# Values phase of a dilated-attention kernel: four token tiles renewed and one key rotation issued later, and the last pair's probabilities read back on SyncE's queue

## The chip, the cores and the metric

The kernel runs on one core of one Trainium2 chip (trn2). The metric is the device time of one execution in microseconds (us); a kernel is timed in several runs and the median counts. A profiled execution is taken beside the timed ones, and all rows of the profile below come from that single execution. Engines are named as the profile names them: PE (TensorE matrix products), PEld (its weight loads), DVE (VectorE), ACT (ScalarE), POOL (GpSimd) and SP (SyncE, which here only issues DMA transfers). Each engine works through its own instructions in the order in which they were placed; they meet through semaphores.

## What is computed

The reference is a two-layer network on 512 tokens of width 1024: dilated attention and a SwiGLU feed-forward layer, then an mLSTM mixer and a second feed-forward layer, with RMS norms. The change touches the attention alone:

```python
proj = (xn @ w_in).reshape(B, S, N_GROUPS, 3, ATTN_HEADS, ATTN_HEAD_DIM)   # 3 groups; q, k, v; 8 heads of 128
for g, (window, dilation) in enumerate(DIL_CONFIGS):                        # (128,1), (512,4), (2048,16)
    q = apply_partial_rope(proj[:, :, g, 0], positions) * scale             # the first 32 of 128 rows are rotated
    k = apply_partial_rope(proj[:, :, g, 1], positions)
    v = proj[:, :, g, 2]
    o, lse = dilated_window_attention(q, k, v, window, dilation)
...
wts = jax.nn.softmax(jnp.stack(lses), axis=0)                               # the three groups share one softmax
o = jnp.einsum('gbsh,gbshd->bshd', wts, jnp.stack(outs))
return o.reshape(B, S, ATTN_WIDTH) @ w_out
```

Here xn is the normalized input; the three groups' results are weighted together, multiplied by w_out and added to the residual h.

## The kernel before

**Products in three parts.** All large products are made with operands split into a high part (fp32r) and a remainder: for a weight tile ACT copies the high part (line 210, tiles ending in _h) and DVE subtracts it from the raw tile (line 211, _l); for activations lines 225/226 and 228/229 do the same. Each product is then three matmuls (`SPLITS`): high times high, low times high, high times low. Every weight goes DMA on SP's queue, then ACT, then DVE, then PE, three buffers deep (`W_BUFS`); `Feed` (line 263) prepares two weight tiles ahead of the one in use.

**Order of the work.** The program is written down in one order, and a scheduler then places each instruction on its engine's list. `behind(fn, engine=...)` and `run(fn)` tie a step's instructions to the last one on an engine; `defer(n, fn)` postpones a step by n ticks, where each chunk of a projection (`project`, line 246) is one tick. So the position of a step in the text moves it on its engine's list, and other instructions may be placed before it.

**First pair's projections.** The eight heads go in four pairs. `project_pair` (line 773) makes q and k of a pair for the three groups. For each, `evac` (line 786) multiplies the accumulator by the cosines (line 790) and shuffles the rows to be rotated out of it (line 574); `rotate` (line 576) multiplies them by the sines (line 577) and adds them (line 582). In pair 0 the tokens are used unnormalized (tiles xa_h, xa_l of x times the gain), and the normalization is applied at each evacuation. While pair 0 is projected, `normalize` writes the normalized tokens to tiles xn, `sum_of` makes the sums S1 to S4 of token blocks, and `renew` (line 828) overwrites the eight operand tiles xa_h (ACT, line 831) and xa_l (DVE, line 832) from xn. `renew(range(4))` is deferred into the last key projection (a0g2k, group 2, part 1); `renew(range(4, 8))` is written right behind that projection, after `rotate` of those keys.

**Values phase.** `values_phase` (line 931) then computes the values of the remaining heads in two units (v0..., v1...). Each unit multiplies tokens by weights through seven block products, in the order P1, P5, P2, P6, P7, P3, P4, each in two halves of 12 matmuls (`multiply_values`, line 974, matmuls on line 982). P1 uses token tiles 0 to 3, P2 tiles 4 to 7, P5 the sum S1. The right-hand sides are made by `prepare_values` (line 903): P5's is W12 - W11, a DVE subtraction on line 907 that must precede ACT's copy (line 210) and DVE's remainder (line 211). `finish` copies accumulators out on ACT (line 939). In the profile v0c is the accumulator of P1 and P2, v0p that of P5, v0u that of P6; the program's weight tiles are v0P_0_h, v0P_1_h and so on (0 and 1 are the halves), their raw tiles v0W. W12 is loaded on SP's queue (line 900) into the place of xn tiles 0 and 1, so its first half waits until tokens 0 and 1 are renewed, its second half for tokens 2 and 3.

**Last pair's attention.** `attention_pair` (line 591) makes the scores, the softmax and the weighting by `joint` and `weigh`. `transposes(i)` (line 730) turns head i's probabilities in blocks on DVE (line 734, tile a3pB for the last pair) and writes them to DRAM (a3pD) in four transfers of 240 KB on POOL's queue (line 737). `bring(i)` (line 740) reads them back as one tile a3pT of 960 KB, also on POOL's queue (line 742). `values(i)` multiplies them (lines 752 and 757, accumulator a3o). In the last pair the steps are, on one tick: `joint` and `weigh(0)`, `transposes(0)`, `bring(0)` and `weigh(1)`, `transposes(1)`, `bring(1)`. A `bring` waits for its head's four writes, and POOL's queue is served in order, so what stands behind it on that queue waits too. Meanwhile PE works on the output product: `out_part` (line 1053) multiplies heads 0 to 5 by w_out (accumulators awo, weights awo_k), then `values(0)`, one more part, `values(1)`, and the rest.

Of the kernel before, what the change touches and what calls it, by code (L numbers as in the profile page):

```python
# [23 lines left out]
HEADS = 8  # L24
# [48 lines left out]
def tile_hybrid_dilated_attn_mlstm(  # L73
# [4 lines left out]
    nc = tc.nc  # L78
    x = x[0]
# [304 lines left out]
    with ExitStack() as actx:  # L384
# [206 lines left out]
        def attention_pair(pr, qks):  # L591
# [6 lines left out]
            p, p0, p12 = [], [], []  # L598
            pts, vt, weight = {}, [], []

            def places():
                p.extend(ap2.tile([P, 15, P], F32, tag="p", name="%sp%d" % (nm, i), bufs=3) for i in range(2))
                p0.extend(t[:, :7] for t in p)
                p12.extend(t[:, 7:] for t in p)
# [45 lines left out]
            def scores12(qk1, qk2):  # L650

                for i in range(2):
                    for g, (q, k) in ((1, qk1), (2, qk2)):
                        sp = score_bank(i, "%ss%d" % (nm, g))
                        for c in range(4):
                            sl = slice(c * P, (c + 1) * P)
                            nc.tensor.matmul(sp[:, sl], q[:, i, sl], k[:, i, sl], start=True, stop=True)
                        for c in range(4):
                            sl = slice(c * P, (c + 1) * P)
                            nc.vector.tensor_tensor_reduce(  # L660
                                p12[i][:, 4 * (g - 1) + c, :], sp[:, sl], mask_causal if g == 1 else mask_dil,
                                1.0, -3e38, op0=ALU.add, op1=ALU.max, accum_out=mx[:, g - 1, i, c:c + 1])
                    exponentials(1, i)
# [73 lines left out]
                    nc.gpsimd.dma_start(d.rearrange("b j a x -> a j b x")[a],  # L737
                                        t[R * a:R * (a + 1)].rearrange("p b n i -> p b (n i)"))

            def bring(i):  # L740
                pt = ap2.tile([P, 4, 15, R], F32, tag="pt", name=nm + "pT", bufs=2)
                nc.gpsimd.dma_start(pt.rearrange("p a n i -> p (a n i)"), pts[i].rearrange("b j a x -> (b j) (a x)"))
                pts[i] = pt

            def values(i, out=None):
# [19 lines left out]
            def first_rest():  # L765
                joint()
                weigh(0)
            rest = (first_rest, lambda: transposes(0), lambda: (bring(0), weigh(1)), lambda: transposes(1),
                    lambda: bring(1))
            return (lambda: (places(), scores0(*qks[0])), lambda: scores12(*qks[1:]), rest, values, load_values,  # L770
                    value_tiles)

        def project_pair(pr, qks, then=None):
            nm = "a%d" % pr
            ct, sines = (ropc, ropes) if pr == 0 else (cosn, sinn)
            late = []
            for g in range(3):
                base = g * 3 * D + pr * 256
                qk = []
                qks.append(qk)  # L780
                for part in range(2):
                    t = tok_tile("%sg%d_%s" % (nm, g, "qk"[part]))

                    sh = ap.tile([R, 2, SEQ], F32, tag="rt", name="rot", bufs=2)

                    def evac(m, acc, t=t, sh=sh, g=g):
                        if g == 0:
                            nc.vector.tensor_tensor(in_order(t[:, m]), by_block(acc), by_block(ct), op=ALU.mult)
                        else:
                            nc.vector.tensor_tensor(t[:, m], acc, ct, op=ALU.mult)  # L790
                        rope_part(sh, m, acc)
                    first = pr == 0 and g == 0 and part == 0
                    if first:
                        def first_evac(evac=evac):
                            bc_hook()
                            for m in range(2):
                                evac(m, facc[m])
                        defer(1, first_evac)
                        late.append((t, sh))
                    else:  # L800
                        if pr == 0 and g == 2 and part == 1:
                            defer(1, lambda: renew(range(4)))
                        project(pair, w_in, base + part * D, KC, evac, "%sg%d%s" % (nm, g, "qk"[part]), ready=feed)
                        while late:
                            rotate(*late.pop(), True, sines)
                        rotate(t, sh, g == 0, sines)
                    qk.append(t)
                    if pr == 0 and 1 <= g:
                        step = 2 * (g - 1) + part
                        (lambda: sum_of("S3"), lambda: sum_of("S4"), lambda: None, lambda: renew(range(4, 8)))[step]()  # L810
                        for key in ((), ("W12", "W22"), (), ())[step]:
                            for hf in range(2):
                                behind(load_block, 0, key, hf, engine=mybir.EngineType.SP)
                if g == 0 and then is not None:
                    then()
                if g == 0 and pr == 0:
                    first_values()
# [113 lines left out]
        def values_phase():  # L931
            bank = lambda tag, name: [ps.tile([P, 512], F32, tag=tag, name=name, bufs=3 if tag == "acc" else 2)
                                      for _ in range(2)]
            target = {"P1": "c11", "P2": "c11", "P5": "p5", "P3": "p5", "P6": "u", "P7": "u", "P4": "u"}
            acc, out = {}, {}

            def copy(to, src):
                for m in range(2):
                    nc.scalar.activation(to[m] if isinstance(to, list) else to[:, m], src[m], AF.Copy)

            def add(to, src):
                for m in range(2):
                    nc.vector.tensor_tensor(to[:, m], src[m], to[:, m], op=ALU.add)

            def stored(u, tile_, half, n):
                nc.gpsimd.dma_start(vD[UNITS[u][n]][half * HALF:(half + 1) * HALF].rearrange("(m p) f -> p m f", p=P), tile_)

            def finish(u, name):
                nm = "v%d" % u
                if name == "P1":  # L950
                    acc["u"] = bank("acc", nm + "u")
                    copy(acc["u"], acc["c11"])
                elif name == "P5":
                    out["v5"] = ap.tile([P, 2, SEQ], F32, tag="rt", name=nm + "v5", bufs=2)
                    copy(out["v5"], acc["p5"])
                elif name == "P6":
                    out["u2"] = ap.tile([P, 2, SEQ], F32, tag="rt", name=nm + "u2", bufs=2)
                    copy(out["u2"], acc["u"])
                elif name == "P2":
                    t = place("st0", nm + "c11")  # L960
                    copy(t, acc["c11"])
                    stored(u, t, 0, 0)
                elif name == "P7":
                    add(out["v5"], acc["u"])
                    stored(u, out["v5"], 1, 1)
                elif name == "P3":
                    add(out["u2"], acc["p5"])
                    stored(u, out["u2"], 0, 1)
                else:
                    t = place("st1", nm + "c21")  # L970
                    copy(t, acc["u"])
                    stored(u, t, 1, 0)

            def multiply_values(u, name, hf):
                nm = target[name]
                if name in ("P1", "P5") and hf == 0:
                    acc[nm] = bank({"c11": "s", "p5": "o"}[nm], "v%d%s" % (u, nm))
                whl = feed.pop()
                for m in range(2):
                    for k in range(2):  # L980
                        for a, b in SPLITS:
                            nc.tensor.matmul(acc[nm][m], left(name, a, 2 * hf + k, m), whl[b][:, k, :],
                                             start=(name in ("P1", "P5") and hf == 0 and k == 0 and (a, b) == SPLITS[0]),
                                             stop=(hf == 1 and k == 1 and (a, b) == SPLITS[-1]), skip_group_check=True)
            for item in items:
                multiply_values(*item)
                if item[2] == 1:
                    finish(*item[:2])

        items = [(u, name, hf) for u in range(len(UNITS)) for name in ORDER for hf in range(2)]  # L990
        plan = [lambda ch=ch: wide_chunk(v12_parts(0), ch, "a0g12v") for ch in range(1, 4)]
# [28 lines left out]
        for pr in range(1, HEADS // 2):  # L1020
# [2 lines left out]
            follow(todo, RUN_AT)  # L1023
            project_pair(pr, qks, lambda fn=following[0]: defer(SCORES0_AT, lambda: run(fn)))
            todo = following
        last_values = todo[3]
        follow(todo, LAST_AT)
        v12 = todo[5]()

# [29 lines left out]

        head_split = lambda k, op: split_act(pair[0][k], pair[1][k], op, None)  # L1060
        for c in range(3):
            out_part(c, feed.pop(), 0)
        whl = [feed.pop() for _ in range(3)]
        for i in range(2):
            out_part(i, whl[i], 1, (0, 1))
# [1061 lines left out]
```

## Time and profile before

| What | Value |
|---|---|
| timed runs | 1399.1, 1401.89, 1403.12 us; median 1401.89 us |
| the profiled execution's own time | 1402.21 us |
| its span, first to last instruction | 1400.3 us |
| mean granted TensorE clock | 0.998 |
| DVE busy | 1120.6 us (80%) |
| ACT busy | 703.1 us (50%) |
| POOL busy | 153.7 us (11%) |
| HBM traffic | 163.63 MB read, 18.87 MB written |

The profile gives busy time by engine, groups of instructions by line, the waits by who ended them, and a timeline in us from the span's start. In a timeline row stand the start, the length, the engine, the line, the operation, output<-inputs, the shapes and a count; in brackets the engine's idle time before it and what ended that. The time of a row xN spans N instructions. DVE and ACT instructions overlap slightly, so the step from one start to the next is shorter than one instruction's length. Buffer numbers are left out of names.

### The profile page before, as it was taken

To read this page: it belongs to the slowest core of one execution; us is meant where nothing else is said; L and a number is where in the kernel's file an instruction comes from. 1 tells how busy PE (TensorE), PEld (TensorE's weight loads), DVE (VectorE), ACT (ScalarE), POOL (GpSimd) and SP (SyncE) were. 2 spreads that over 40 slices of the span, in tenths; PEclk is the share of its full clock that TensorE was granted. 3 is DMA by queue.
4 is the path that set the end of the run, shared out by engine and by line. 5 is a ranking of instruction groups with operands and counts; after the bars stand their busy time and mean duration, and the time that the engine had idled before them with its cause. 6 is when DMAs were issued, how large, how long until landed. Compare 5 with 4: busy or idle time off the path is not lost. (4 is left out here: it accounts for less than half of the span.)

```text
span 1400.3 us, 21529 instructions
## 1 busy us (share of the span) xinstructions
PE 1381.8 (99%) x8308; PEld 1232.1 (88%) x8308; DVE 1120.6 (80%) x1904; ACT 703.1 (50%) x1153; POOL 153.7 (11%) x225
## 2 busy tenths in 40 slices
PE   9999999999999999999999999999999999999997
PEld 7887888888888888999999998898888899999886
DVE  7977769596867299877877898898858987888887
ACT  5325552132325155445566464786534544458854
POOL 1000011111010000000000100113101230001212
PEclk9999999999999999999999999999999999999999
DMA  7533255537262547333253643324334563335963
GB/s 226 165 120 106 99 157 174 150 111 213 88 193 80 181 137 164 121 121 109 92 166 87 156 131 91 92 77 106 97 116 117 136 190 121 121 108 134 196 164 100
DMA packets 136830, 186.00 MB, mean 133 GB/s; under 512 B 8532, under 2 KB 104340, under 8 KB 136728
## 3 DMA queue, kind: packets, MB, share of 16 engines
q1 hardware_dynamic: 117312, 134.17, 30.9%
q0 software_dynamic: 17760, 49.34, 15.3%
q8 instruction: 65, 1.06, 0.3%
q10 hardware_dynamic: 1656, 1.12, 0.2%
q14 instruction: 37, 0.30, 0.1%
HBM read 163.63 MB, written 18.87 MB: 130 GB/s over the span
## 5 line engine op out<-in xcount | busy, mean ns | idle before, releaser
L1430 POOL DMA_DIRECT2D f1T<-in_ffn_w_out_dram x15 | 17.8, 1185 | 209.3 <-DMA f1P_2w_w<-in_ffn_w_out_dram 136.6
L1405 POOL DMA_DIRECT2D f0S<-in_ffn_w_out_dram x10 | 8.7, 891 | 244.8 <-DMA f0S<-in_ffn_w_out_dram 190.9
L1962 POOL DMA_DIRECT2D hD<-hB x32 | 21.7, 697 | 68.4 <-DVE hB L1959 68.4
L241 PE MATMUL mo<-n_h,mo_k_l 128*128 128x512 f32 x64 | 25.3, 396 | 0.0
L241 PE MATMUL mo<-n_h,mo_k_h 128*128 128x512 f32 x64 | 25.2, 394 | 0.0
L241 PE MATMUL mo<-n_l,mo_k_h 128*128 128x512 f32 x64 | 25.2, 394 | 0.0
L241 PE MATMUL mqk<-n_h,mqk_k_h 128*128 128x512 f32 x64 | 25.1, 393 | 0.0
L241 PE MATMUL mwo<-yo_l,mwo_k_h 128*128 128x512 f32 x64 | 25.1, 392 | 0.0
L241 PE MATMUL awo<-ao_h,awo_k_h 128*128 128x512 f32 x64 | 25.1, 392 | 0.0
L241 PE MATMUL mqk<-n_l,mqk_k_h 128*128 128x512 f32 x64 | 25.1, 392 | 0.0
L241 PE MATMUL f1j<-n_h,f1j_h 128*128 128x512 f32 x64 | 25.0, 391 | 0.0
L241 PE MATMUL f0j<-n_h,f0j_h 128*128 128x512 f32 x64 | 25.0, 391 | 0.0
L241 PE MATMUL mwo<-yo_h,mwo_k_l 128*128 128x512 f32 x64 | 25.0, 391 | 0.0
L241 PE MATMUL mqk<-n_h,mqk_k_l 128*128 128x512 f32 x64 | 25.0, 390 | 0.0
L241 PE MATMUL f0j<-n_h,f0j_l 128*128 128x512 f32 x64 | 24.9, 390 | 0.0
L241 PE MATMUL f1j<-n_h,f1j_l 128*128 128x512 f32 x64 | 24.9, 390 | 0.0
L241 PE MATMUL awo<-ao_h,awo_k_l 128*128 128x512 f32 x64 | 24.9, 389 | 0.0
L241 PE MATMUL f0j<-n_l,f0j_h 128*128 128x512 f32 x64 | 24.9, 389 | 0.0
L241 PE MATMUL f1j<-n_l,f1j_h 128*128 128x512 f32 x64 | 24.9, 389 | 0.0
L241 PE MATMUL awo<-ao_l,awo_k_h 128*128 128x512 f32 x64 | 24.9, 389 | 0.0
L241 PE MATMUL mwo<-yo_h,mwo_k_h 128*128 128x512 f32 x64 | 24.8, 391 | 0.0
L211 DVE TENSOR_TENSOR v1P_l<-v1W,v1P_h 128x1024 fp32r<-128x1024 f32 x14 | 17.1, 1224 | 9.6 <-ACT v1P_h L210 9.6
(2492 smaller groups left out, 5670.5 us busy)
## 6 DMA issues: line engine op xcount, KB each, us to landing
f0j_w<-in_ffn_w_in_dram SPq DMA_DIRECT2D x17, 512.0 KB, 5.5
f1j_w<-in_ffn_w_in_dram SPq DMA_DIRECT2D x17, 512.0 KB, 6.1
f1T<-in_ffn_w_out_dram POOLq DMA_DIRECT2D x15, 512.0 KB, 7.6
f0hid<-in_ffn_w_in_dram SPq DMA_DIRECT2D x9, 512.0 KB, 5.7
f1hid<-in_ffn_w_in_dram SPq DMA_DIRECT2D x9, 512.0 KB, 5.2
v0W<-in_attn_w_in_dram SPq DMA_DIRECT2D x8, 512.0 KB, 5.3
v1W<-in_attn_w_in_dram SPq DMA_DIRECT2D x8, 512.0 KB, 4.0
awo_k_w<-in_attn_w_out_dram SPq DMA_DIRECT2D x8, 512.0 KB, 5.0
```

Of the source, the lines that this page charges most:

```text
L211: nc.vector.tensor_tensor(lo[:, :n], raw[:, :n], hi[:, :n].bitcast(F32), op=ALU.subtract)
L241: nc.tensor.matmul(acc, whl[a][:, k, m * P:(m + 1) * P], pairs[b][kk], start=(kk == 0 and (a, b) == SPLITS[0]), stop=(kk == nk - 1 and (a, ...
L1405: nc.gpsimd.dma_start(t, src[1][:, ks], accum_op=ALU.add)
L1430: nc.gpsimd.dma_start(view(to), weight_rows(hk * UNITS + u, n), accum_op=ALU.add)
L1962: nc.gpsimd.dma_start(hD[k // 4].rearrange("(b i) x -> i b x", i=R)[:, :, c0:c0 + R], t[R * a_:R * (a_ + 1)])
```

## The change

The change has three parts. The renewal of token tiles 4 to 7 moves from behind the last key projection to behind the first item of the values phase (P1's first half). The rotation of the last keys (group 2 of pair 0) moves behind the fourth item (P5's second half). In the last pair the five steps become one that leaves out both `bring`; these are called while the output product's first halves are started, `bring(0)` ahead of the second and `bring(1)` ahead of the third, and go on SP's queue.

```diff
--- before.py
+++ after.py
@@ -737,9 +737,9 @@
                     nc.gpsimd.dma_start(d.rearrange("b j a x -> a j b x")[a],
                                         t[R * a:R * (a + 1)].rearrange("p b n i -> p b (n i)"))
 
-            def bring(i):
+            def bring(i, queue=nc.gpsimd):
                 pt = ap2.tile([P, 4, 15, R], F32, tag="pt", name=nm + "pT", bufs=2)
-                nc.gpsimd.dma_start(pt.rearrange("p a n i -> p (a n i)"), pts[i].rearrange("b j a x -> (b j) (a x)"))
+                queue.dma_start(pt.rearrange("p a n i -> p (a n i)"), pts[i].rearrange("b j a x -> (b j) (a x)"))
                 pts[i] = pt
 
             def values(i, out=None):
@@ -767,8 +767,12 @@
                 weigh(0)
             rest = (first_rest, lambda: transposes(0), lambda: (bring(0), weigh(1)), lambda: transposes(1),
                     lambda: bring(1))
+            if pr == HEADS // 2 - 1:
+                rest = (lambda: (first_rest(), transposes(0), weigh(1), transposes(1)),)
             return (lambda: (places(), scores0(*qks[0])), lambda: scores12(*qks[1:]), rest, values, load_values,
-                    value_tiles)
+                    value_tiles, bring)
+
+        postponed = []
 
         def project_pair(pr, qks, then=None):
             nm = "a%d" % pr
@@ -803,11 +807,14 @@
                         project(pair, w_in, base + part * D, KC, evac, "%sg%d%s" % (nm, g, "qk"[part]), ready=feed)
                         while late:
                             rotate(*late.pop(), True, sines)
-                        rotate(t, sh, g == 0, sines)
+                        if pr == 0 and g == 2 and part == 1:
+                            postponed.append(lambda: rotate(t, sh, False, sines))
+                        else:
+                            rotate(t, sh, g == 0, sines)
                     qk.append(t)
                     if pr == 0 and 1 <= g:
                         step = 2 * (g - 1) + part
-                        (lambda: sum_of("S3"), lambda: sum_of("S4"), lambda: None, lambda: renew(range(4, 8)))[step]()
+                        (lambda: sum_of("S3"), lambda: sum_of("S4"), lambda: None, lambda: None)[step]()
                         for key in ((), ("W12", "W22"), (), ())[step]:
                             for hf in range(2):
                                 behind(load_block, 0, key, hf, engine=mybir.EngineType.SP)
@@ -982,10 +989,14 @@
                             nc.tensor.matmul(acc[nm][m], left(name, a, 2 * hf + k, m), whl[b][:, k, :],
                                              start=(name in ("P1", "P5") and hf == 0 and k == 0 and (a, b) == SPLITS[0]),
                                              stop=(hf == 1 and k == 1 and (a, b) == SPLITS[-1]), skip_group_check=True)
-            for item in items:
+            for i, item in enumerate(items):
                 multiply_values(*item)
                 if item[2] == 1:
                     finish(*item[:2])
+                if i == 0:
+                    renew(range(4, 8))
+                if i == 3:
+                    postponed.pop()()
 
         items = [(u, name, hf) for u in range(len(UNITS)) for name in ORDER for hf in range(2)]
         plan = [lambda ch=ch: wide_chunk(v12_parts(0), ch, "a0g12v") for ch in range(1, 4)]
@@ -1023,7 +1034,7 @@
             follow(todo, RUN_AT)
             project_pair(pr, qks, lambda fn=following[0]: defer(SCORES0_AT, lambda: run(fn)))
             todo = following
-        last_values = todo[3]
+        last_values, last_bring = todo[3], todo[6]
         follow(todo, LAST_AT)
         v12 = todo[5]()
 
@@ -1059,7 +1070,10 @@
 
         head_split = lambda k, op: split_act(pair[0][k], pair[1][k], op, None)
         for c in range(3):
-            out_part(c, feed.pop(), 0)
+            whl = feed.pop()
+            if c:
+                last_bring(c - 1, nc.sync)
+            out_part(c, whl, 0)
         whl = [feed.pop() for _ in range(3)]
         for i in range(2):
             out_part(i, whl[i], 1, (0, 1))
```

## Prediction

> **What bounds the kernel now.** I read the page first, for the engine with the largest share.
>
> ```profile
> PE 1381.8 (99%) x8308; PEld 1232.1 (88%) x8308; DVE 1120.6 (80%) x1904; ACT 703.1 (50%) x1153; POOL 153.7 (11%) x225
> ```
>
> PE is the bound: it is idle for only 1400.3 - 1381.8 = 18.5 us. A change that leaves the matmuls alone can win only idle time, or time in which PE runs below its clock. So the second view is the list of PE's waits, and three of its longest lie in the two stages that the change touches.
>
> ```profile
> PE v0p L982 <- ACT v0P_h L210: 1.7, 1, 1.7
> ...
> PE a3o L752 <- DMA a3pT<-a3pD: 1.4, 1, 1.4
> PE v0c L982 <- ACT v0P_h L210: 1.3, 1, 1.3
> ```
>
> The third view is the busy time in three stretches: P1, then P5 with P2, then P6 with P7 (PE, PEld, DVE, ACT, POOL, clock, DMA share, GB/s).
>
> ```profile
> 100.89:106.33 5.44, 5.44 (x25) 4.32 (x23) 5.44 (x9) 1.37 (x3) 0.00 (x0) 1.00 0.67 258
> 106.33:122.27 15.94, 12.88 (x50) 10.10 (x49) 14.63 (x14) 8.50 (x10) 0.00 (x0) 0.89 0.01 2
> 122.27:139.00 16.73, 16.73 (x74) 13.61 (x73) 9.91 (x10) 7.93 (x9) 1.43 (x2) 1.00 0.68 201
> ```
>
> P1's 24 matmuls take 5.44 us, 0.227 us each. P5 and P2 have 48, which at that rate need 10.88 us; they take 15.94. **5.06 us are lost there**: 15.94 - 12.88 = 3.06 us idle, 15.94 x 0.11 = 1.75 us by the lower clock, the rest in restarting. What PE waits for is read from the timelines of DVE, ACT and PE.
>
> ```profile
> 98.50 0.67 DVE L790 TENSOR_TENSOR a0g_k<-a0g2k,ropc 128x512 f32<-128x512 f32 x1
> ...
> 99.75 1.34 DVE L832 TENSOR_TENSOR xa_l<-xn,xa_h 128x512 fp32r<-128x512 f32 x2
> 101.09 0.69 DVE L790 TENSOR_TENSOR a0g_k<-a0g2k,ropc 128x512 f32<-128x512 f32 x1
> ...
> 102.33 0.66 DVE L832 TENSOR_TENSOR xa_l<-xn,xa_h 128x512 fp32r<-128x512 f32 x1
> 102.92 1.21 DVE L577 TENSOR_TENSOR rot<-rot,rops 32x1024 f32<-32x1024 f32 x1
> 104.06 0.67 DVE L832 TENSOR_TENSOR xa_l<-xn,xa_h 128x512 fp32r<-128x512 f32 x1
> 104.66 1.21 DVE L582 TENSOR_TENSOR a0g_k<-a0g_k,rot 32x1024 f32<-32x1024 f32 x1
> 105.79 3.48 DVE L907 TENSOR_TENSOR v0W<-v0W,v0W 128x1024 f32<-128x1024 f32 x3
> 109.20 3.48 DVE L211 TENSOR_TENSOR v0P_l<-v0W,v0P_h 128x1024 fp32r<-128x1024 f32 x3
> ```
>
> ```profile
> 99.05 2.67 ACT L831 ACTIVATE xa_h<-xn 128x512 fp32r<-128x512 f32 x4 [1.98 <-PE a0g2k L241]
> 105.17 0.58 ACT L939 ACTIVATE v0u<-v0c 128x512 f32<-128x512 f32 x1 [3.45 <-PE v0c L982]
> 106.53 0.58 ACT L939 ACTIVATE v0u<-v0c 128x512 f32<-128x512 f32 x1 [0.78 <-PE v0c L982]
> 107.09 3.14 ACT L210 ACTIVATE v0P_h<-v0W 128x1024 fp32r<-128x1024 f32 x3
> ```
>
> ```profile
> 108.20 0.73 PE L982 MATMUL v0p<-v0P_h,S 128*128 128x512 f32 x2 [1.71 <-ACT v0P_h L210]
> 110.29 1.22 PE L982 MATMUL v0c<-v0P_h,xa_h 128*128 128x512 f32 x2 [1.35 <-ACT v0P_h L210]
> ```
>
> P5's first right-hand side is subtracted (line 907) only at 105.79, behind the four xa_l and the rotation; ACT copies it at 107.09, behind two accumulator copies; PE gets it at 108.20, although P1 was over at 106.33.
>
> **First and second part: renewal and rotation.** No instruction is added or taken away. The order of the changed program on DVE, from 98.50 on, is: cosine product and shuffle (as before), *line 907 for P5's first half*, one xa_l, cosine product, shuffle, *remainder P5 first half*, three xa_l, line 907 for P5's second half, line 577, line 907 for P6, remainder P5 second half, both remainders of P2, line 582. On ACT the copy for P5's first half stands ahead of the two accumulator copies. Steps from start to start come from the rows: cosine product 0.61 (to 99.11), shuffle 0.64, xa_l 0.59, lines 577 and 582 1.14, the 1024-wide 907 and 211 (109.20 - 105.79)/3 = 1.14; ACT's 1024-wide copy 1.05.
>
> The moved subtraction needs W12's first half, and DVE, serving in order, holds everything behind it until that has landed. The load's issue, and its nearest kin with a landing time, its second half:
>
> ```profile
> 96.26 0.37 SPq L900 DMA_DIRECT2D v0W<-in_attn_w_in_dram  x1
> ```
>
> ```profile
> v0W<-in_attn_w_in_dram SPq DMA_DIRECT2D x1, 512.0 KB, 4.1
> ```
>
> ```profile
> DMA to landing us min/median/max: 4.1/5.1/6.2
> ```
>
> The issue does not move. With 4.1 us it lands at 100.4, with the longest of the v0W loads (6.2) at 102.5, and at no price if before 99.75. I take 100.4. Then DVE runs: 907 to 101.54, xa_l 102.13, cosine product 102.74, shuffle 103.38, remainder 104.52, three xa_l 106.30, 907 for P5's second half 107.44, 577 108.58, 907 for P6 109.72, remainder P5 second half 110.86, P2's 112.00 and 113.14, 582 114.28. ACT copies P5's first half at 101.7, the accumulators as before, P5's second half from 107.5 to 108.6, P2's first from 108.6 to 109.65.
>
> PE: P1 ends at 106.33 and P5's first half (ready 104.5) follows without a gap to 109.05. The next four matmuls in its order need two ACT copies, 108.6 and 109.65: a wait of 0.15. Then the remainder at 110.95: at 110.1 PE waits 0.85. P5's other ten end at 113.2, P2's (remainders 112.1 and 113.2) at 118.2. Later splits come earlier too: P6's remainder at about 116.5. PE's stall is thus 1.0 us, and I add 0.1 for restarting: lost 1.1 instead of 5.06, **a gain of 4.0 us**. From 99.75 to 100.4 DVE's own wait is inside this. The rotation, taken off the path, is needed first by the scores after the values phase, tens of us later.
>
> The clock: I keep it at 1.00, because one idle stretch of this length exists at full clock, the wait of a3o (column 1.00 below). The Trainium skill, "TensorE: Matmul & The Clock Gate", section "Why this matters for your kernels", puts the limit at idle gaps of about 3 us; by that the first part keeps its 4.0 us. The row of 106.33 shows the clock falling with gaps of 1.71 and 1.35 us; the measurement decides, and two shorter waits may be enough again (first rival).
>
> **Third part: the read-back.** Rows of POOL's and SP's issues, of their landing times, and of PE:
>
> ```profile
> 457.78 0.55 POOL L737 DMA_DIRECT2D a3pD<-a3pB  x1 [2.82 <-DVE a3pB L734]
> 459.95 0.56 POOL L742 DMA_DIRECT2D a3pT<-a3pD  x1 [1.62 <-DMA a3pD<-a3pB]
> 460.50 1.64 POOL L737 DMA_DIRECT2D a3pD<-a3pB  x3
> 470.84 0.56 POOL L742 DMA_DIRECT2D a3pT<-a3pD  x1 [8.70 <-DMA a3pD<-a3pB]
> ```
>
> ```profile
> a3pT<-a3pD POOLq DMA_DIRECT2D x1, 960.0 KB, 8.1
> ...
> a3pT<-a3pD POOLq DMA_DIRECT2D x1, 960.0 KB, 5.0
> ```
>
> ```profile
> 462.02 0.37 SPq L202 DMA_DIRECT2D awo_k_w<-in_attn_w_out_dram  x1
> ...
> 467.41 0.37 SPq L202 DMA_DIRECT2D f0j_w<-in_ffn_w_in_dram  x1
> ```
>
> ```profile
> awo_k_w<-in_attn_w_out_dram SPq DMA_DIRECT2D x1, 512.0 KB, 9.2
> ```
>
> ```profile
> 467.59 0.39 PE L241 MATMUL awo<-ao_h,awo_k_l 128*128 128x512 f32 x1
> 468.12 1.80 PE L752 MATMUL a3o<-a3pT,a3v 128*128 128x128 f32 x14
> ...
> 474.07 0.39 PE L241 MATMUL awo<-ao_h,awo_k_l 128*128 128x512 f32 x1
> 475.90 1.83 PE L752 MATMUL a3o<-a3pT,a3v 128*128 128x128 f32 x14 [1.44 <-DMA a3pT<-a3pD]
> ```
>
> ```profile
> 466.00:468.00 2.00, 1.98 (x9) 1.31 (x7) 1.23 (x1) 0.13 (x1) 0.00 (x0) 1.00 0.98 395
> ...
> 474.00:476.00 2.00, 0.56 (x4) 0.14 (x2) 0.00 (x0) 0.00 (x0) 0.00 (x0) 1.00 0.52 219
> ```
>
> Before, PE loses 468.12 - (467.59 + 0.23) = 0.30 us to the first read-back (landed at 459.95 + 8.1 = 468.05) and 475.90 - (474.07 + 0.23) = 1.60 to the second: 1.90 in all. After, the second head's four writes leave POOL from 457.78 on, 0.55 apart, with no read-back between; all are issued by 459.99. The read-backs stand on SP's list behind the last awo load and behind the first f0j load. So **the first is issued later**, 462.02 + 0.37 = 462.4, the second earlier, 467.8.
>
> First read-back: alone it would take 5.0 (its twin), landing at 467.4; if it fares like the load ahead of it, 9.2, and 448 KB more at 395 GB/s = 1.1, it lands at 472.7. The truth is near the low end, as its own queue's 512 KB ahead cost 1.3 us at 395 GB/s and a rest of the second head's writes some 0.4: 469.1, matmuls at 469.2, lost 1.4 instead of 0.3. Second: 467.8 + 5.0 + 1.3 for the f0j load ahead = 474.1; PE wants it 474.30 - 468.12 = 6.2 us after the first, at 475.4. So its 1.60 us go. **Gain 1.9 - 1.4 = 0.5 us** (bounds +1.9 and, at 472.7, -3.1). Behind the read-backs SP's f0j loads wait 0.4 us each for issue; they feed the next stage's product, and the rest of the output product, at least PE's rows from 474.07 on, hides that.
>
> The Trainium skill, "Trainium Kernel Development and Optimization", section "Key Constraints", says that transfers of all queues share the same 16 DMA engines, so another issuing queue saves only issue time. By that nothing is faster here, and the first read-back's later issue is the whole effect; the row with 9.2 us agrees that the queues delay each other.
>
> **Sum.** 4.0 + 0.5 = 4.5 us. The profiled execution's own time is 1402.21, its span 1400.3 with 1.9 around it, which stays: 1397.7. The median of the runs is 0.3 below that execution, so 1397.4; I forecast **1397.5 us**. The 4.0 us won at 118 persist because PE is busy throughout between there and the end, and what feeds it is released by its own progress; in the 16.73 us after 122.27 DVE works only 9.91.
>
> **Rivals.**
> - *The clock falls again.* Two waits in 1.5 us, at 109.5 and 110.1, could suffice. Before, the clock lost 1.75 us; that taken from 4.5 gives 1399.5. For it: 1.71 and 1.35 did it. Against: 1.44 alone did not.
> - *DVE held at its head.* W12's half lands at 102.5: 2.1 us later in every DVE step, so 2.1 us more stall: 1399.6.
> - *Both read-backs land in time*, the first at 467.4: third part 1.9, time 1396.1.
> - *Slower than before: the first read-back sits behind other queues as the awo load did.* Landing at 472.7 loses 5.0 us, long enough for the lower clock (1.75): 1.9 - 5.0 - 1.75 = -4.85, against 4.0: 0.9 us slower, 1402.8. It turns slower from a landing at about 471.9. For it: 9.2 us in that place. Against: the transfer that held that load was the very read-back, then on the other queue.
> - *The gain is not kept*, since a later stage is paced by DVE or a transfer: about 1401.5. Against: no PE wait between 123 and 467 appears among the longest.
>
> **How the numbers follow.** Forecast 0.60 (its own range 1396.3 to 1399.0), clock 0.12, DVE held 0.08, both in time 0.10, slower 0.05, not kept 0.05. From these the range is 1395.3 to 1400.5: it takes in the clock, the held DVE and the read-backs in time. A measurement here tells 0.3%, 4.2 us, from no change, so faster means under 1397.8; the forecast lies at that edge. Faster: 0.10 and two thirds of 0.60, 0.50; same 0.46; slower by so much, 0.04.
>
> **What would show it.** First part right: line 907 starts on DVE near 100.4, PE's stretch from P1's end to P6's start is near 12 us at clock 1.00, and no wait there passes 1 us. Wrong: a DVE wait for a v0W transfer of over 1 us, or a clock under 1.00. Third part: the first a3pT is issued right behind the last awo load and PE waits more than 0.3 us for it, the second not at all. Wrong, if the first wait passes 3 us, or the second stays.

## The result, and the profile after

The changed kernel took 1398.87 us (median of 22 runs, 1397.05 to 1400.23) where the kernel before took 1401.97 on the same chip: a ratio of 0.9977, 95% interval 0.997 to 0.9985, so 2.1 to 4.2 us less. Its profiled execution took 1398.66 us with a span of 1396.7. The total is near the forecast; its terms are not. Two windows per kernel show that: from the first matmul of P1 to the first of P6, and from the first awo matmul to the first matmul of the next layer (f0j). The kernel before (columns as in the prediction: PE, PEld, DVE, ACT, POOL, clock, DMA share, GB/s):

```profile
100.88:122.26 21.38, 18.32 (x73) 14.41 (x72) 20.07 (x22) 9.87 (x13) 0.00 (x0) 0.92 0.17 67
448.77:501.15 52.38, 50.79 (x253) 42.59 (x252) 27.73 (x42) 17.37 (x24) 5.50 (x10) 1.00 0.51 157
```

The changed kernel:

```profile
100.53:117.38 16.85, 16.62 (x74) 13.44 (x72) 16.85 (x20) 9.68 (x13) 0.00 (x0) 1.00 0.21 80
443.90:498.93 55.03, 52.16 (x253) 44.30 (x252) 27.74 (x42) 17.37 (x24) 4.39 (x8) 0.97 0.48 149
```

The **values window** gained 21.38 - 16.85 = 4.53 us; the **output window** lost 55.03 - 52.38 = 2.65. Between them nothing moved (448.77 - 122.26 = 326.51, 443.90 - 117.38 = 326.52). The two windows make 1.88 of the 3.6 us by which the spans differ; 0.35 lie ahead of P1 and 1.38 behind 500. A second profile of the changed kernel (below) has the same windows, but 0.62 and -0.07 in those two places, so one pair of profiles can't say whether they belong to the change.

Where the values window won: DVE in the changed kernel (line 914 is line 907 of before, 839 is 832).

```profile
99.41 1.23 DVE L914 TENSOR_TENSOR v0W<-v0W,v0W 128x1024 f32<-128x1024 f32 x1
...
102.39 1.20 DVE L211 TENSOR_TENSOR v0P_l<-v0W,v0P_h 128x1024 fp32r<-128x1024 f32 x1
103.52 1.88 DVE L839 TENSOR_TENSOR xa_l<-xn,xa_h 128x512 fp32r<-128x512 f32 x3
105.33 1.21 DVE L914 TENSOR_TENSOR v0W<-v0W,v0W 128x1024 f32<-128x1024 f32 x1
...
108.73 3.48 DVE L211 TENSOR_TENSOR v0P_l<-v0W,v0P_h 128x1024 fp32r<-128x1024 f32 x3
```

P5's first half is subtracted at 99.41 with no idle time before it (no bracket), so W12's half had landed by then; its remainder is ready at 103.5, before P1 ends. P5 and P2 take 11.43 us at full clock, and PE waits once:

```profile
105.97:117.40 11.43, 11.20 (x50) 8.95 (x49) 11.43 (x11) 7.36 (x9) 0.00 (x0) 1.00 0.00 1
```

```profile
109.99 0.50 PE L989 MATMUL v0p<-v0P_l,S 128*128 128x512 f32 x1 [0.23 <-DVE v0P_l L211]
```

Where the output window lost: SP's issues of the changed kernel, the longest wait of its queue between 440 and 475 (us in total, times, longest), the first read-back's time to landing, the stretch from its issue to its landing (DMA share 0.99), then PE.

```profile
450.56 6.96 SPq L202 DMA_DIRECT2D awo_k_w<-in_attn_w_out_dram  x3
457.81 1.68 SPq L742 DMA_DIRECT2D a3pT<-a3pD  x1
462.54 0.37 SPq L202 DMA_DIRECT2D f0j_w<-in_ffn_w_in_dram  x1
463.08 0.38 SPq L742 DMA_DIRECT2D a3pT<-a3pD  x1
```

```profile
SPq L202 <- DVE awo_k_l L211: 17.7, 4, 9.1
```

```profile
a3pT<-a3pD SPq DMA_DIRECT2D x1, 960.0 KB, 8.0
```

```profile
457.81:465.83 8.02, 5.29 (x24) 4.05 (x22) 1.23 (x1) 1.06 (x1) 0.00 (x0) 1.00 0.99 345
```

```profile
462.71 0.39 PE L241 MATMUL awo<-ao_h,awo_k_l 128*128 128x512 f32 x1
465.97 2.22 PE L752 MATMUL a3o<-a3pT,a3v 128*128 128x128 f32 x14 [2.87 <-DMA a3pT<-a3pD]
467.98 3.21 PE L757 MATMUL a3o<-a3pT,a3v 128*128 128x128 f32 x16
...
473.79 1.72 PE L752 MATMUL a3o<-a3pT,a3v 128*128 128x128 f32 x14
```

The first read-back stands behind three awo loads that wait for their buffers (DVE's remainders); it goes out at 457.81 and lands 8.0 us later. PE, free at 462.94, starts at 465.97: 3.03 us lost instead of 0.30. The second needs no wait (1.60 won). Then comes a loss that the list of waits doesn't have. The clock by stretches of 3.41 us, changed kernel first, then the kernel before in the values phase:

```profile
463.77:467.18 3.41, 1.21 (x11) 1.24 (x12) 0.00 (x0) 0.00 (x0) 0.00 (x0) 1.00 0.99 340
467.18:470.59 3.41, 3.41 (x19) 3.41 (x18) 0.00 (x0) 0.00 (x0) 0.00 (x0) 0.50 0.46 190
```

```profile
106.49:109.90 3.41, 0.73 (x2) 0.30 (x2) 3.41 (x4) 3.29 (x4) 0.00 (x0) 1.00 0.01 2
109.90:113.32 3.42, 3.03 (x7) 2.46 (x8) 3.42 (x4) 0.33 (x1) 0.00 (x0) 0.50 0.02 5
```

The half clock that the change removed at 110 us comes back at 467, right behind the read-back's wait. Of the 2.65 us, the waits make 3.03 - 1.90 = 1.13; the other 1.52 is put down to the half clock. Half of 3.41 us would be 1.71, and two profiles of part3 below, with the same wait, differ by 1.67 with and without it.

### The profile page after: what moved, and what is told of

Same layout as the page of the kernel before. It is cut to its first block, busy times and chain, and to the rows that moved or that the text cites. A ratio compares the mean times of both kernels' runs of the same rounds, so it can differ in the third digit from the quotient of the medians.

```text
span 1396.7 us, 21529 instructions
## 1 busy us (share of the span) xinstructions
PE 1380.6 (99%) x8308; PEld 1232.4 (88%) x8308; DVE 1120.2 (80%) x1904; ACT 703.0 (50%) x1153; POOL 153.7 (11%) x223
```

## The experiments

**Theory 1**: the first two parts keep their 4.5 us; the third loses, because SP's list issues the first read-back late, and through the half clock behind the wait. **Theory 2**: the third part is free and the gain is eaten later. **Theory 3**: the read-back is late because of the second head's writes on the shared DMA engines, whatever the queue. All kernels' windows in us (the stretch from a3g12v to f0j of some expectations is 0.15 shorter than the output window), and their ratios to the kernel before, run on the same chip:

| kernel | values | output | ratio (95% interval) |
|---|---|---|---|
| before | 21.38 | 52.38 | |
| changed, changed_again, changed_look | 16.85, 16.88, 17.23 | 55.03, 55.05, 54.91 | 0.9977 (0.997 to 0.9985), 0.998 (0.9971 to 0.9989), none |
| parts12 | 17.16 | 52.26 | 0.9976 (0.9963 to 0.9989) |
| part3, part3_look | 21.58, 21.28 | 53.40, 55.07 | 1.0011 (1.0001 to 1.0021), none |
| pool_order | 17.05 | 52.16 | 0.9968 (0.9956 to 0.9979) |
| sync_forced | 17.17 | 50.30 | 0.9956 (0.994 to 0.9971) |
| sync_first | 16.84 | 50.88 | 0.9958 (0.9946 to 0.9971) |
| part3_forced | 19.96 | 50.91 | 0.9986 (0.9973 to 0.9998) |
| renewal_only | 19.11 | 52.10 | 0.9986 (0.9976 to 0.9996) |
| swapped_look | 17.12 | 60.13 | none |

**parts12**, the third part undone:

```diff
-            if pr == HEADS // 2 - 1:
-                rest = (lambda: (first_rest(), transposes(0), weigh(1), transposes(1)),)
...
-            whl = feed.pop()
-            if c:
-                last_bring(c - 1, nc.sync)
-            out_part(c, whl, 0)
+            out_part(c, feed.pop(), 0)
```

> Only the first two parts: renewal and rotation as in the changed kernel, the read-backs of the last pair on GpSimd's queue as before. Theory 1 (the change's third part loses about 2.75 us: the first read-back waits 2.9 us of PE time in place of 0.3 and the clock falls behind that wait, for 1.6 us; the second read-back's wait of 1.6 us goes): the first two parts keep the whole 4.5 us that their stretch shows, so this kernel takes 1397.4 us by the medians (1401.97 less 4.5), about 1.5 us under the changed kernel or more, with a PE wait of about 0.3 us ahead of the first a3o matmuls and 1.6 us ahead of the second, and no granted clock of half speed in either place. Theory 2 (the third part costs nothing and about a fifth of the first two parts' gain is lost later): about 1398.9 us, the changed kernel's time.

Measured: 1397.41 us against 1400.91. Both windows:

```profile
100.73:117.89 17.16, 16.62 (x73) 13.38 (x72) 17.16 (x20) 9.76 (x13) 0.00 (x0) 1.00 0.22 84
444.36:496.62 52.26, 50.78 (x253) 42.58 (x252) 27.73 (x42) 17.37 (x24) 5.53 (x10) 1.00 0.51 157
```

The values window keeps the gain (4.2 here), and the output window is that of before. So the windows give all of the gain to the first two parts. The medians can't tell this kernel from the changed one (3.5 us under before against 3.1), although the windows say 2.5 us. The interval of 1.8 us to each side is part of it. Two more things on record bear on it, and neither is tested by a run of its own:
- The granted clock varies between timed runs of one kernel: beside parts12, eight runs of the kernel before with a mean clock of 0.999 average 1399.4 us, five with 0.996 average 1402.7. So the windows of one profile need not be the median's. The six runs of parts12 at 0.999 average 1396.7, 2.7 us less.
- Behind the output window, the four profiles with the read-backs on POOL take 898.8 to 899.6 us (mean 899.1), the nine with read-backs on SP 897.8 to 899.2 (mean 898.2). The third part may win some of the missing time there; the groups overlap, and it isn't shown.

The rest stays open.

**part3**, only the third part (renewal and rotation put back where they were), and the same kernel again as **part3_look**.

> Only the third part: the read-backs of the last pair on SyncE's queue, renewal and rotation as before. Theory 1: the stretch of values keeps its half clock, and PE waits 2.9 us ahead of the first a3o matmuls and loses 1.6 us more behind it by the clock, less 1.9 us for the second read-back and its restart: about 1404.7 us, 2 to 3 us above the kernel before. Theory 2: 1402 us, the time before. The prediction's own price of this part (a gain of 0.5) would give 1401.5.

> The third part alone once more, for its profile only. Theory 1a (a wait of 2.9 us brings the half clock, and the first profile of it was the exception): 3.41 us at half clock behind the wait, stretch from a3g12v to f0j about 54.9 us. Theory 1b (the fall comes in some executions only, or not so soon after the fall at 110 us): no half clock there, about 53.2 us again.

Measured: 1402.69 against 1400.91, slower by 0.0011 (interval 0.1 to 2.9 us). The wait is 2.9 us in both profiles, but the output window is 53.40 in one and 55.07 in the other. In the first no half clock followed (rows two and three are the stretches that hold the wait; the stretches are counted in steps of 3.41 us from the fall at 110.20, row one being the stretch ahead of it):

```profile
106.78:110.20 3.42, 1.58 (x6) 1.02 (x7) 3.42 (x4) 2.44 (x3) 0.00 (x0) 1.00 0.01 2
...
465.18:468.60 3.42, 2.02 (x9) 1.33 (x8) 1.23 (x1) 0.18 (x1) 0.00 (x0) 1.00 0.93 335
468.60:472.01 3.41, 1.93 (x17) 1.96 (x18) 0.00 (x0) 0.00 (x0) 0.00 (x0) 1.00 0.95 341
472.01:475.42 3.41, 3.41 (x24) 3.07 (x24) 0.69 (x1) 0.60 (x1) 0.00 (x0) 1.00 0.25 103
```

In part3_look the wait lies in one stretch, and the next is at half clock:

```profile
468.11:471.52 3.41, 0.77 (x7) 0.80 (x8) 0.00 (x0) 0.00 (x0) 0.00 (x0) 1.00 0.99 342
471.52:474.93 3.41, 3.41 (x19) 3.41 (x18) 0.00 (x0) 0.00 (x0) 0.00 (x0) 0.50 0.53 215
```

Theory 2 falls: the third part costs 1.0 us without the half clock and 2.7 with it. What decides between these is taken up with changed_look.

**pool_order**, the changed kernel with `last_bring(c - 1, nc.gpsimd)`.

> As the changed kernel, but the two read-backs on GpSimd's queue, both behind the eight writes of the two heads (in the kernel before the first stood behind four of them). It tells SyncE's queue from the order of reads and writes. Theory 1 (what makes the first read-back late is its place on SyncE, behind the last load for the output projection, which waits for its buffer until 456.9 us of the changed kernel's span): it is issued some 2 us earlier, about 455, lands at 463 to 464, and PE waits under 1.5 us; about 1396.5 us. Theory 3 (late because the second head's writes run ahead of it on the shared DMA engines, whatever the queue): it lands at about 465.6 still, PE waits about 3 us, and the time is the changed kernel's, 1398.9 us.

Measured: 1396.89 us against 1400.91. POOL's issues, and the first read-back's time to landing:

```profile
452.72 2.18 POOL L737 DMA_DIRECT2D a3pD<-a3pB  x4 [2.82 <-DVE a3pB L734]
454.88 0.56 POOL L742 DMA_DIRECT2D a3pT<-a3pD  x1
```

```profile
a3pT<-a3pD POOLq DMA_DIRECT2D x1, 960.0 KB, 9.5
```

```profile
464.54 1.80 PE L752 MATMUL a3o<-a3pT,a3v 128*128 128x128 f32 x14 [1.64 <-DMA a3pT<-a3pD]
```

Issued 2.7 us earlier than on SP (the output window begins at 443.70, 0.2 ahead of the changed kernel's), it lands 1.2 us earlier, since it takes 9.5 us instead of 8.0 with the second head's four writes ahead of it on the queue: in the trace its first packet starts 4.5 us after its issue, against 2.0 in sync_forced below, and its packets then take 4.8 us, against 5.8. Theory 1 holds for the larger part; theory 3 for 1.5 us, on this queue.

**sync_forced**, both read-backs on SP, with the place forced:

```diff
+        with tc.issue_after(ahead[name]) if name in ahead else nullcontext():
-        nc.sync.dma_start(view(raw), src)
+            nc.sync.dma_start(view(raw), src)
...
                 last_bring(c - 1, nc.sync)
+                ahead[("awo3_k0", "f0j0_00")[c - 1]] = last_on(mybir.EngineType.SP)
```

> As the changed kernel, both read-backs on SyncE's queue, but ordered there by hand: the first ahead of the last two loads for the output projection, the second ahead of the first load of the next layer. Theory 1: the first is issued when its head's writes have landed, about 454.3 us, and lands about 8 us later, at 462.3 to 463, the second at 461 and lands by 469; PE waits under 0.6 us at the first and not at the second, no half clock in either place; about 1395.5 us, the least of all. Theory 3: the read-back shares the DMA engines with the second head's writes and lands at 464 or later; PE waits 1.5 to 3 us and the time is 1397 to 1399 us.

Measured: 1394.68 us against 1400.91, the fastest of all kernels. SP's issues, PE, and the windows:

```profile
454.31 0.34 SPq L745 DMA_DIRECT2D a3pT<-a3pD  x1
454.75 2.56 SPq L205 DMA_DIRECT2D awo_k_w<-in_attn_w_out_dram  x2
462.23 0.34 SPq L745 DMA_DIRECT2D a3pT<-a3pD  x1
```

```profile
462.74 1.72 PE L755 MATMUL a3o<-a3pT,a3v 128*128 128x128 f32 x14
...
468.87 1.72 PE L755 MATMUL a3o<-a3pT,a3v 128*128 128x128 f32 x14
```

```profile
100.01:117.18 17.17, 16.65 (x73) 13.41 (x72) 17.17 (x20) 9.77 (x13) 0.00 (x0) 1.00 0.22 84
443.70:494.00 50.30, 50.30 (x253) 42.74 (x252) 27.74 (x42) 17.37 (x24) 4.39 (x8) 1.00 0.52 163
```

PE is busy through the whole output window. The windows' gain, 4.21 + 2.08 = 6.3 us, is the median's, 6.2. The first read-back's last packet ends at 462.07, 7.8 us after its issue, beside the same writes on the other queue.

**sync_first**, the same with the first read-back alone forced.

> As the run with both read-backs ordered by hand on SyncE, but only the first is put ahead of the last two loads for the output projection; the second stays behind the first load of the next layer, as in the changed kernel. Theory 1: the first read-back's place is the whole loss, the second's costs nothing (it would land at about 469, and PE needs it at about 470): 1394.7 us against a kernel before of 1400.9, ratio 0.9956, as with both. Rival: the second lands 1 to 2 us too late behind that load, and half the gain over GpSimd's queue goes: ratio 0.997.

Measured: 1395.12 us against 1401.61. The second read-back is 0.33 us late and the window 0.58 longer; the ratios agree within their intervals. The first one's place is what counts.

**part3_forced**, this order with renewal and rotation as before.

> The third part alone, with both read-backs ordered by hand on SyncE as in the run with both forced (the first ahead of the last two loads for the output projection, the second ahead of the first load of the next layer); renewal and rotation as before. Theory 1 (only the place of the first read-back on SyncE makes the third part lose): the stretch from a3g12v to f0j takes about 50.1 us, 2.1 less than before, while P5 and P2 keep their waits: ratio 0.9985, about 2 us under the kernel before. Rival (the third part only pays once the first two have gained, for then everything is earlier): no gain, ratio 1.000.

Measured: 1399.27 us against 1401.7. The output window is 50.91 here too: the third part, well placed, gains without the first two. The values window is 19.96, although it has the waits of before: no half clock followed them, so the 1.42 us won there (21.38 - 19.96) are no gain of the third part. The stretches are counted back from the fall at the end of this trace, 1390.87.

```profile
104.05:107.47 3.42, 1.71 (x9) 1.09 (x7) 3.42 (x4) 2.24 (x4) 0.00 (x0) 1.00 0.00 1
107.47:110.88 3.41, 2.06 (x8) 1.41 (x9) 3.41 (x4) 1.97 (x2) 0.00 (x0) 1.00 0.03 7
110.88:114.29 3.41, 3.41 (x17) 2.82 (x16) 3.41 (x4) 1.45 (x2) 0.00 (x0) 1.00 0.00 0
```

**renewal_only**, the first part alone.

```diff
-                        if pr == 0 and g == 2 and part == 1:
-                            postponed.append(lambda: rotate(t, sh, False, sines))
-                        else:
-                            rotate(t, sh, g == 0, sines)
+                        rotate(t, sh, g == 0, sines)
...
-                if i == 3:
-                    postponed.pop()()
```

> The renewal alone, rotation and read-backs as before. The order on VectorE moves the subtraction for P5's first half forward as in the changed kernel, but the rotation (lines 577 and 582) stays ahead of the subtraction for P5's second half, and the remainder of that half is taken behind two more subtractions. Theory 1 (the gain needs both parts): PE has P5's first half without a wait, but the second half's remainder comes about 112.1 us, when PE could use it at about 109: 2.4 to 3.4 us lost of the 4.2 to 4.7 gained, a time 1 to 2 us under the kernel before. Rival (the renewal alone carries the gain, since rotation is only 2.3 us of VectorE): about 4 us under the kernel before, as the first two parts together.

Measured: 1398.99 us against 1401.61. The values window wins 2.27 of 4.53 us. P5's second half is what stays late:

```profile
103.85 1.21 DVE L577 TENSOR_TENSOR rot<-rot,rops 32x1024 f32<-32x1024 f32 x1
...
105.59 1.21 DVE L582 TENSOR_TENSOR a0g_k<-a0g_k,rot 32x1024 f32<-32x1024 f32 x1
...
107.93 3.47 DVE L909 TENSOR_TENSOR v0W<-v0W,v0W 128x1024 f32<-128x1024 f32 x3
```

```profile
110.34 0.74 PE L984 MATMUL v0p<-v0P_h,S 128*128 128x512 f32 x2 [1.15 <-ACT v0P_h L210]
111.29 0.74 PE L984 MATMUL v0c<-v0P_h,xa_h 128*128 128x512 f32 x2 [0.21 <-ACT v0P_h L210]
112.59 0.50 PE L984 MATMUL v0p<-v0P_l,S 128*128 128x512 f32 x1 [0.57 <-DVE v0P_l L211]
```

Its subtraction (line 909 here) comes at 107.93 instead of 105.33 (P1 starts 0.34 later in this execution), and PE waits three times. So half of the gain comes with the renewal, the other half only with both. The rotation alone, with the renewal where it was, was not run; its list on DVE is another again (all four xa_l, then both subtractions for P5, then line 577), so what it gains by itself isn't shown.

**changed_again** and **changed_look**, the changed kernel; **swapped_look**, with the second head's read-back issued ahead of the first's:

```diff
-                last_bring(c - 1, nc.sync)
+                with tc.issue_after(last_on(mybir.EngineType.SP)) if c == 2 else nullcontext():
+                    last_bring(2 - c, nc.sync)
```

> The changed kernel once more, beside the others on one chip, for two open points: its ratio against the first two parts alone (0.9976 elsewhere), and whether the granted clock falls behind the wait ahead of the first a3o matmuls. In its first profile a wait of 2.87 us was followed by 3.41 us at half clock; with the third part alone a wait of 2.9 us was followed by none. Theory 1a (the fall belongs to the wait): half clock again at about 467 us, the stretch from the last matmul on a3g12v to the first on f0j about 54.9 us, and a time some 2.7 us above that of the first two parts alone. Theory 1b (the fall comes in some executions only): none this time, that stretch about 53.2 us, 1.0 us above the kernel before, and a time about 1 us above that of the first two parts alone. The ratio is 0.997 to 0.9985 either way.

> The changed kernel once more, for its profile, at another position of the slots. With the slots: the idle time of about 3 us ahead of the first a3o matmuls leaves PE busy less than half of one slot of 3.41 us in about nine positions of ten (not where the wait is split about evenly between two slots), so half clock for 3.41 us right behind that slot, and the stretch from a3g12v to f0j 54.9 us; if the two slots that hold the wait both show more than about 1.7 us of busy PE, no half clock and about 53.2 us. By chance alone the fall would bear no relation to these shares.

> As the changed kernel, but the second head's read-back is issued ahead of the first's on SyncE, so that the one that PE needs first lands last: the suspected wait doubled. From the profiles so far: the granted clock stands in slots of 3.41 us, and a slot in which PE was busy for 1.58 us or less was followed by a slot at half clock, one in which it was busy 1.78 us or more was not. Theory 1a', with the slots: the wait is 6 to 7 us (landing about 469.5 instead of 465.6), at least one slot is idle for more than half wherever the slots lie, and the half clock is certain, for one slot of work or two; the stretch from a3g12v to f0j takes 58 to 60.5 us. Theory 1b (the fall comes by chance): it may stay away behind a longer wait too, and the stretch then takes about 56.7 us.

Measured: half clock behind the wait again in both, windows of 55.05 and 54.91. But the median of changed_again, 1398.47 against 1401.61, isn't the 2.7 us above parts12 that theory 1a asks for. The first row is the stretch ahead of the fall in changed_look:

```profile
462.66:466.07 3.41, 0.66 (x5) 0.27 (x4) 0.00 (x0) 0.00 (x0) 0.00 (x0) 1.00 0.96 348
466.07:469.49 3.42, 3.42 (x18) 3.42 (x18) 0.00 (x0) 0.00 (x0) 0.00 (x0) 0.50 0.72 280
```

With the read-backs swapped, PE waits 7.8 us (6 to 7 expected), the half clock lasts two stretches, and the output window is 60.13:

```profile
465.12:468.53 3.41, 0.00 (x0) 0.00 (x0) 0.00 (x0) 0.00 (x0) 0.00 (x0) 1.00 1.07 426
468.53:471.95 3.42, 0.35 (x2) 0.38 (x3) 0.00 (x0) 0.00 (x0) 0.00 (x0) 0.50 0.64 265
471.95:475.36 3.41, 3.41 (x18) 3.41 (x17) 0.00 (x0) 0.00 (x0) 0.00 (x0) 0.50 0.00 0
475.36:478.77 3.41, 3.41 (x23) 3.07 (x23) 0.69 (x1) 0.60 (x1) 0.00 (x0) 1.00 0.02 5
```

So it is neither the wait's length alone nor chance. In every row here, a stretch with PE busy 1.58 us or less (1.58, 1.21, 0.77, 0.73, 0.66, 0.35, 0.00) is followed by one at half clock, a stretch with 1.71 or more (1.71, 1.93, 2.02, 2.06) is not: the bound lies near half of 3.41 us. The same holds throughout all thirteen traces: in each, the clock changes only at whole multiples of 3.41 us from its first change, the busiest stretch ahead of a half clock has 1.58 us, and the idlest ahead of a full one 1.7. Where a wait falls on these stretches differs from execution to execution, so a wait of 2.7 to 2.9 us brought the half clock in four profiles of five, and the waits of P5 and P2 in three of four.

## Why the prediction was right and where it failed

- **First and second part, right.** The order on DVE and ACT came as stated. Predicted 4.0 us, measured 4.53. The difference is W12's landing: I took 100.4 (100.05 in this execution, which is 0.35 ahead), line 907 (914 now) started at 99.41, so everything behind it came 0.6 earlier, and of the waits of 0.15 and 0.85 only 0.23 was left.
- **The clock in the values phase, right for a reason that was too simple.** It stayed at 1.00. I argued from one wait at full clock; the runs show that PE's busy share of a 3.41 us stretch decides. It also makes the gain vary: of 4.53 us, about 1.4 is the half clock, which part3_forced didn't have.
- **The gain is kept, right.** 326.5 us from P6 to the output product in both.
- **Third part, wrong in size and sign.** Predicted a gain of 0.5, measured a loss of 2.65. The step that failed is "the truth is near the low end": the issue was right (462.4 foretold, 457.81 + 4.87 = 462.7 in the time of before), but the landing was 470.7, not 469.1. I started from 5.0 us, the second read-back's time, and added 1.3 and 0.4 for what stood ahead; that addition measured 3.0 instead of 1.7. From issue to its last packet the first one takes 7.5 to 8.2 us on either queue in every profile but pool_order (9.3) and swapped_look, while the second head's writes, awo loads and it fill the DMA engines (share 0.99 in the row at 457.81). The row with 8.1 us, on POOL before, was shown, and should have been the base. The second failed step is the clock, left at 1.00 behind a wait that I had at 1.4 and that was 2.9.
- **The second read-back**, right: no wait, 1.60 us won.
- **The slower rival** named the right mechanism, late read-back and then the lower clock, with 5.0 and 1.75 us; it came with 3.03 and 1.52, a net loss of 2.65, less than the 4.53 won. On its own, in part3, it made the kernel slower. (A sum beside it is off: 1.75 us more than 1397.5 is 1399.25, not the 1399.5 of the first rival.)
- **The total.** 1397.5 forecast, 1398.87 measured: clear of no change, but above the 1397.8 under which I spoke of faster. That it lies so near is partly luck. The windows alone, 1.88 us under 1401.97, would have given 1400.1; it lies nearer because the medians differ by 3.1 us, 1.2 more than the two windows account for, and that rest stays open. The first part, with 0.5 more than I said, made up for a little of what the third lost.
- **The two rules cited.** The Trainium skill, "TensorE: Matmul & The Clock Gate", section "What's actually happening", tells of a free-running window of 3413 ns; the runs agree with it (half clocks of 3.41 and 6.83 us). The limit of about 3 us for an idle gap that the Trainium skill gives on the same page, section "Why this matters for your kernels", and that I weighed, is too generous here: 3.41 - 0.73 = 2.68 us of idle, in two waits, did it at 106.49, and 3.41 - 1.58 = 1.83 us at 106.78 in part3. The Trainium skill, "Trainium Kernel Development and Optimization", section "Key Constraints", says that another issuing queue saves only issue time; for the main effect that holds, but with issue times 0.57 us apart, the read-back took 9.3 us to its last packet behind the writes on their queue and 7.8 on the other.

## What to carry to other kernels

A transfer moved to another queue inherits what stands ahead of it there and what that waits for: read the target list, and force the place if the scheduler doesn't give it (1394.68 against 1398.87 us by order alone, each beside its own before of 1400.91 and 1401.97). For its duration, use the row of the same transfer in the same traffic, not that of its twin in quiet. Two waits inside one stretch of 3.41 us count together for the clock, so a wait has a second price, 1.67 us where two profiles show it alone, that depends on where it falls; add it wherever PE may idle more than about half of such a stretch.

## What the runs showed of the hardware beyond that

I hadn't expected that one program with one wait has two times: part3 and part3_look are the same kernel with the same wait of 2.9 us, and their output windows differ by 55.07 - 53.40 = 1.67 us, by where the wait lay on the clock's stretches of 3.41 us. I also hadn't expected that the same read-back, issued within 0.57 us of the same moment, takes 9.3 us to its last packet on the queue that carries the other head's writes and 7.8 beside it.
